# Strassen's weight sums in a transformer trunk: from VectorE to ScalarE negations and adding DMAs

## The chip, the cores and the metric

The kernel runs on one core of one Trainium2 chip. The metric is the device time of one execution in microseconds, as the median of several runs. The engines are TensorE (PE for its matmuls, PEld for its weight loads), VectorE (DVE), ScalarE (ACT), GpSimd (POOL) and SyncE (SP), which here only issues DMAs.

## The reference, cut to what matters

The reference is a trunk of two layers on 256 tokens of width 2048. Each layer has a mixer (attention of two kinds) and then a feed-forward block. The change touches only the feed-forward block:

```python
h = rms_norm(x, norm_mlp[i])
x = x + jnp.square(jax.nn.relu(h @ w_up[i])) @ w_down[i]
```

`w_up[i]` is 2048 x 8192, `w_down[i]` is 8192 x 2048, all in float32.

## The kernel before

**The stream of items.** The whole kernel is one list of items. An item is one block of weights of 256 rows by 512 columns (two row blocks of 128, held as a tile of 128 x 1024 elements, 512 KB) and the matmuls that use it. For each item the main loop (the end of `trunk`) does three things ahead of time. `load` issues, from SyncE, the DMA of the block into a tile `wraw` out of a ring of 5, seven items ahead. `split`, two items ahead, writes the block as the sum of two parts of reduced precision into a tile `w` out of a ring of 3: the high part by a ScalarE copy (`copy`, L89), the low part by a VectorE subtraction (L993). Then `mm` issues the matmuls, three for each product of 128 rows (high x high, high x low, low x high). An item whose `src` is empty is not loaded; its `form` says which tile is split instead. `early`, `after` and `post` are lists of further steps that are issued before an item's matmuls, after its split, and after its matmuls.

Since `w` has three buffers, the split of an item can begin when the matmuls three items before it are done.

**The down projection.** The hidden width of 8192 is taken in four parts f = 0 to 3 of 2048. For each f, `up(f)` computes the hidden features (lines L289 to L291, 16 items of 256 rows for each of four column blocks), and `down(f)` multiplies them with the rows of `w_down` of this part. `down(f)` takes the 2048 output columns in two pairs n = 0, 1 of two blocks G and H of 512 columns (`down_pair`). In the order of the program up(f + 1) stands before down(f). In the second layer the last pair (f = 3, n = 1) is done by plain items, so there are 15 pairs in all, 8 in the first layer and 7 in the second.

In each pair, six of the eight row blocks are plain: items G0 to G5 and H0 to H5 of 12 matmuls each (L427). The other two row blocks, `qa` and `qb` (0 and 2), form with the two column blocks and the two token blocks a 2 x 2 by 2 x 2 product, computed by Strassen's scheme in a form due to Winograd: seven items s1 to s7 of six matmuls each (`seventh`, L446) instead of eight. Four of them multiply blocks of w_down as they are, b11 (rows qa, columns G), b12 (qa, H), b21 (qb, G), b22 (qb, H), or sums of them:

| item | weights |
|---|---|
| s1, s2, s3 | b11, b21, b22 |
| s5 | b12 - b11 up to sign |
| s7 | b22 - b12 up to sign |
| s6 | b11 + b22 - b12 up to sign |
| s4 | b21 - (s6's sum) up to sign |

The left factors are blocks of the hidden features or sums of them, which `sums` computes on VectorE ahead of each f. The results of s5, s6, s7 and s1 are added to the residual `xs` by VectorE (`p1` to `p7`, L466, L482). Those of s2, s3 and s4 go on top of the sums of the plain items.

The order of the items in a pair is written out by hand:

```python
TURNS = "G0 s1 G1 H0 s5 G2 H1 s7 G3 H2 G4 s6 H3 s3 s2 H4 s4 G5 H5".split()
```

**The block sums before.** `load_block` loads b11, b22, b21 and b12 from SyncE into four tiles of their own, issued 8, 6, 5 and 3 items before the pair begins. When an s item is split, `minus` (L489) first makes the difference of two blocks on VectorE, in place of one of them, and `b4` (L494) makes the one for s4 after the split of s6. The s items read these tiles, so they have no `wraw` of their own.

Within the down projection instructions that go through `keep` stay in program order on their engine; for the others the scheduler of the framework picks the order on each engine when the program is built, so that an instruction may stand earlier than it was written. The matmuls' order is fixed.

## Time and profile before

| | |
|---|---|
| median of 3 runs | 2077.85 us (2077.53 to 2077.92) |
| the profiled execution's own time | 2077.52 us |
| its span | 2075.8 us |
| TensorE busy | 2062.2 us (99%) |
| VectorE busy | 1467.0 us (71%) |
| ScalarE busy | 1026.2 us (49%) |
| GpSimd busy | 26.3 us (1%) |
| granted TensorE clock | 1.00 |
| read from HBM | 425.90 MB |

A row of a timeline gives start, duration, engine, line, operation, output and inputs, the number of instructions merged into it, and in brackets how long the engine was idle before and what ended that. PE and PEld are TensorE's matmuls and weight loads. A row of the waits gives the waiting engine and line, what it waited for, the total in us, how often, and the longest. In the tables by line a bar separates busy time and mean duration (in ns) from the idle time before. Transfers are told by the median time from issue to landing. The ends of matmuls are modelled, so how long a matmul really occupied TensorE is seen from the distance of the starts.

In rows on the order of instructions, numbers behind a tile's name tell buffers apart, sizes are partitions x elements, and semaphores in brackets are what an instruction waits for: DMASW for transfers issued by GpSimd, DMAHW for those of SyncE, and the engines by name.

### The profile page before, as it was taken

What the parts mean: (1) busy time and instruction counts of PE and PEld (TensorE: products, weight loads), DVE (VectorE), ACT (ScalarE), POOL (GpSimd) and SP (SyncE); (2) the same over time, 40 slices, a digit from 0 to 9 for tenths busy, and PEclk for the clock granted to TensorE, in tenths of its full rate; (3) what the DMA queues carried; (4) which work ended last, traced back from release to release, by engine and by line L of the source; (5) the groups of instructions that cost most, each with busy time, mean ns of one, the idle gap of its engine ahead of it and who ended that gap; (6) DMA issues with size and microseconds to landing.
All of it is one profiled execution on the core that took longest, in us unless ns stands there. A gap on an engine that the chain in (4) does not pass through costs nothing.

```text
span 2075.8 us, 24805 instructions
## 1 busy us (share of the span) xinstructions
PE 2062.2 (99%) x9164; PEld 1696.1 (82%) x9164; DVE 1467.0 (71%) x1611; ACT 1026.2 (49%) x1233; POOL 26.3 (1%) x71
## 2 busy tenths in 40 slices
PE   9999999999999999999999999999999999999999
PEld 7888888888888888888887788878888888888887
DVE  5556555666696687688885898666669668867885
ACT  6555554544444454445554566554445444444453
POOL 0100000000000000000000000000000000000000
PEclk9999999999999999999999999999999999999999
DMA  9787856988766966876679688498876687677655
GB/s 305 229 235 213 236 172 199 298 250 245 219 208 216 256 206 209 233 211 209 200 216 264 184 250 258 143 265 271 246 242 205 212 238 221 209 216 224 204 176 165
DMA packets 477466, 464.83 MB, mean 224 GB/s; under 512 B 269665, under 2 KB 279969, under 8 KB 477345
## 3 DMA queue, kind: packets, MB, share of 16 engines
q1 hardware_dynamic: 469488, 455.81, 72.3%
q10 hardware_dynamic: 7856, 7.45, 1.2%
q8 instruction: 71, 1.16, 0.2%
q14 instruction: 51, 0.41, 0.1%
HBM read 425.90 MB, written 37.22 MB: 223 GB/s over the span
## 4 chain that ended last, share of the span: by engine, by line
PE 88%; DVE 6%; DMA 2%; issue 2%; ACT 1%; SPq 1%; DVEq 0%; ACTq 0%
PE acc L290 20%; PE acc L291 20%; PE acc L289 20%; PE acc L427 19%; DVE w L993 3%; PE aux L446 2%; DVE xs L466 2%; PE acc L446 1%; ACT w L89 1%; SPq L175 1%; DMA td<-jx 1%; PE acc L259 1%; PE aux L858 1%; DMA wraw<-in_w_up_dram 1%; DVE u L482 0%
## 5 line engine op out<-in xcount | busy, mean ns | idle before, releaser
L993 DVE TENSOR_TENSOR w<-wraw,w 128x1024 fp32r<-128x1024 f32 (+1 forms) x680 | 826.8, 1217 | 506.8 <-ACT w L89 502.0
L89 ACT ACTIVATE w<-wraw 128x1024 fp32r<-128x1024 f32 (+1 forms) x680 | 720.5, 1060 | 860.4 <-PE acc L291 565.0
L290 PE MATMUL acc<-w,xT 128*128 128x512 f32 x1632 | 638.1, 391 | 1.7 <-DVE w L993 1.5
L289 PE MATMUL acc<-w,xT 128*128 128x512 f32 x1632 | 637.1, 391 | 1.9 <-ACT xT L200 1.0
L291 PE MATMUL acc<-w,xT 128*128 128x512 f32 x1632 | 636.3, 390 | 0.0
L427 PE MATMUL acc<-w,hT 128*128 128x512 f32 x2160 | 512.3, 390 | 4.4 <-DVE w L993 3.4
L427 PEld LDWEIGHTS acc<-w,hT 128*128 128x128 f32 x2160 | 404.0, 188 | 96.1 <-DVE w L993 12.4
L289 PEld LDWEIGHTS acc<-w,xT 128*128 128x128 f32 x1632 | 306.4, 188 | 66.8 <-ACT w L89 2.1
L290 PEld LDWEIGHTS acc<-w,xT 128*128 128x128 f32 x1632 | 306.4, 188 | 66.5 <-DVE w L993 2.7
L291 PEld LDWEIGHTS acc<-w,xT 128*128 128x128 f32 x1632 | 306.4, 188 | 64.1 <-issue 0.7
L89 ACT ACTIVATE w<-b 128x1024 fp32r<-128x1024 f32 x105 | 111.5, 1062 | 83.9 <-PE acc L427 61.1
L993 DVE TENSOR_TENSOR w<-b,w 128x1024 fp32r<-128x1024 f32 x105 | 127.8, 1217 | 26.8 <-ACT w L89 26.8
L289 PE MATMUL acc<-w,oT 128*128 128x512 f32 x256 | 100.3, 394 | 0.0
L290 PE MATMUL acc<-w,oT 128*128 128x512 f32 x256 | 99.5, 390 | 0.0
L291 PE MATMUL acc<-w,oT 128*128 128x512 f32 x256 | 99.0, 391 | 0.0
L446 PE MATMUL aux<-w,S 128*128 128x512 f32 x270 | 68.5, 389 | 0.0
L446 PEld LDWEIGHTS aux<-w,S 128*128 128x128 f32 x270 | 50.7, 188 | 10.5
L289 PEld LDWEIGHTS acc<-w,oT 128*128 128x128 f32 x256 | 48.1, 188 | 10.2 <-ACT junk L796 0.4
L290 PEld LDWEIGHTS acc<-w,oT 128*128 128x128 f32 x256 | 48.1, 188 | 9.8
L291 PEld LDWEIGHTS acc<-w,oT 128*128 128x128 f32 x256 | 48.1, 188 | 9.8
L489 DVE TENSOR_TENSOR b<-b,b 128x1024 f32<-128x1024 f32 x45 | 54.8, 1217 | 0.2
L169 DVE STREAM_TRANSPOSE jx<-acc 128x512 f32<-128x512 f32 x68 | 44.6, 694 | 12.0 <-PE acc L291 9.2
(176 smaller groups left out, 1200.0 us busy)
## 6 DMA issues: line engine op xcount, KB each, us to landing
wraw<-in_w_up_dram SPq DMA_DIRECT2D x256, 512.0 KB, 4.4
wraw<-in_w_down_dram SPq DMA_DIRECT2D x196, 512.0 KB, 4.7
wraw<-in_w_in_a_dram SPq DMA_DIRECT2D x94, 512.0 KB, 4.6
wraw<-in_w_in_b_dram SPq DMA_DIRECT2D x64, 512.0 KB, 4.6
td<-jx SPq DMA_DIRECT2D x240, 128.0 KB, 4.3
b<-in_w_down_dram SPq DMA_DIRECT2D x60, 512.0 KB, 4.9
jx<-td SPq DMA_DIRECT2D x45, 512.0 KB, 6.1
wraw<-in_w_out_a_dram SPq DMA_DIRECT2D x32, 512.0 KB, 3.7
```

Source lines behind the costliest of these rows:

```text
L89: pin(act.activation(o, i, AF.Copy, scale=scale))
L169: dve.transpose(y[:, m:m + k, :].rearrange("p k f -> p (k f)"), part)
L175: keep(nc.sync.dma_start(d[:, :, :, a, :].rearrange("b j n i -> j n b i"), y[32 * a:32 * a + 32].rearrange("p n (b i) -> p n b i", b=4)))
L259: pin(pe.matmul(accs[key][t], L[:, j, part, t * P:(t + 1) * P], wx[:, j, :], start=(j == 0 and n == 0), stop=False))
L289: pin(pe.matmul(acc[t], L[:, k, 0, ts], wh[:, j, :], start=(k == 0), stop=False))
L290: pin(pe.matmul(acc[t], L[:, k, 0, ts], wl[:, j, :], start=False, stop=False))
L291: pin(pe.matmul(acc[t], L[:, k, 1, ts], wh[:, j, :], start=False, stop=(k == (end if t else KT) - 1)))
L427: keep(pe.matmul(acc[t], L[:, k, part, ts], wx[:, j, :], start=(i, j, m) == (0, 0, 0), stop=(i, j, m) == (len(qs) - 1, KB - 1, 2)))
L446: keep(pe.matmul(p, left(part, j), wx[:, j, :], start=to is None and (j, m) == (0, 0), stop=to is None and (j, m) == (KB - 1, 2)))
L466: dve.scalar_tensor_tensor(xc, p, sec["rs2"][:, t:t + 1], xc, op0=OP.mult, op1=OP.add)
L489: dve.tensor_sub(x, block(a), block(b))
L993: pin(dve.tensor_sub(wl[:, a], raw[:, a], wh[:, a].bitcast(F32)))
```

## The change

The sums of weight blocks are made in another way. For each pair there are two tiles, tx and ty, in two sets for n = 0 and n = 1 (the same room as the four tiles before).

- s1, s2 and s3 become ordinary items: their blocks come in the stream of `wraw`.
- 11 items before the pair, SyncE loads b12 into ty (`load_block`). At 8 items, ScalarE writes -ty into tx and then -ty into ty (`negate`, an ACTIVATE with scale -1). At 7 items, two DMAs issued by GpSimd with an accumulate operation add b11 to tx and b22 to ty, from DRAM (`gather`). tx is then s5's sum and ty s7's.
- After the split of s7, another adding DMA adds b11 to ty, which makes s6's sum.
- After the split of s6, ScalarE writes -ty into tx, and an adding DMA adds b21: s4's sum.
- In `sums`, the signs of two left blocks are turned (two `scalar_tensor_tensor` in place of an add and a subtraction), since the signs of the weight sums differ from before.

The items, their order and the matmuls are the same. The core of the diff:

```diff
-        def load_block(name, f, n, col, q):
-            b = sec[name, n % 2] = sec["pool"].tile([P, KB, 512], F32, name=name, bufs=1)
-            nc.sync.dma_start(b, rows(w_down[l], 2048 * f + KB * P * q, KB * P,
-                                      1024 * n + 512 * col, 512))
+        def block_rows(f, n, col, q):
+            return rows(w_down[l], 2048 * f + KB * P * q, KB * P, 1024 * n + 512 * col, 512)
...
-            dve.tensor_add(b4[:, 0], a21, a22)
-            dve.tensor_sub(b4[:, 1], b4[:, 0], a11)
+            dve.scalar_tensor_tensor(b4[:, 0], a21, -1.0, a22, op0=OP.mult, op1=OP.subtract)
+            dve.scalar_tensor_tensor(b4[:, 1], b4[:, 0], -1.0, a11, op0=OP.mult, op1=OP.subtract)
...
-                it = Item(None, KB, 512, mm, True)
-                it.form = form
+                it = Item(None if callable(form) else form, KB, 512, mm, True)
+                it.form = form if callable(form) else None
...
-            def minus(out, a, b, then=None):
-                def form():
-                    x = block(out)
-                    dve.tensor_sub(x, block(a), block(b))
-                    return x
-                return form
-
-            def b4():
-                dve.tensor_sub(block("b12"), block("b21"), block("b11"))
-
             qa, qb = SEVEN
+
+            def raw(col, q):
+                return block_rows(f, n, col, q)
+
+            def load_block():
+                for name in ("tx", "ty"):
+                    sec[name, half] = sec["pool"].tile([P, KB, 512], F32, name=f"{name}{half}", bufs=1)
+                nc.sync.dma_start(block("ty"), raw(1, qa))
+
+            def negate(out, i):
+                act.activation(block(out), block(i), AF.Copy, scale=-1.0)
+
+            def gather(out, col, q):
+                nc.gpsimd.dma_start(block(out), raw(col, q), accum_op=OP.add)
+
+            def t1_t3():
+                negate("tx", "ty")
+                negate("ty", "ty")
+
+            def add_t1_t3():
+                gather("tx", 0, qa)
+                gather("ty", 1, qb)
+
+            def t4():
+                negate("tx", "ty")
+                gather("tx", 0, qb)
+
             seven = {
-                "s1": seventh(own(qa, 0), lambda: block("b11"), None, p1),
-                "s2": seventh(own(qb, 0), lambda: block("b21"), (0, 0)),
-                "s3": seventh(summed(3), lambda: block("b22"), (1, 0)),
-                "s4": seventh(own(qb, 1), lambda: block("b12"), (0, 1)),
-                "s5": seventh(summed(0), minus("b11", "b12", "b11"), None, p5),
-                "s6": seventh(summed(1), minus("b11", "b22", "b11"), None, p6),
-                "s7": seventh(summed(2), minus("b12", "b22", "b12"), None, p7)}
-            seven["s6"].after = b4
+                "s1": seventh(own(qa, 0), raw(0, qa), None, p1),
+                "s2": seventh(own(qb, 0), raw(0, qb), (0, 0)),
+                "s3": seventh(summed(3), raw(1, qb), (1, 0)),
+                "s4": seventh(own(qb, 1), lambda: block("tx"), (0, 1)),
+                "s5": seventh(summed(0), lambda: block("tx"), None, p5),
+                "s6": seventh(summed(1), lambda: block("ty"), None, p6),
+                "s7": seventh(summed(2), lambda: block("ty"), None, p7)}
+            seven["s7"].after = lambda: gather("ty", 0, qa)
+            seven["s6"].after = t4
...
-            for name, col, q, at in (("b11", 0, qa, 8), ("b22", 1, qb, 6), ("b21", 0, qb, 5), ("b12", 1, qa, 3)):
-                items[base - at].early.append(lambda name=name, col=col, q=q: load_block(name, f, n, col, q))
+            for at, step in ((11, load_block), (8, t1_t3), (7, add_t1_t3)):
+                items[base - at].early.append(step)
```

In the changed kernel the lines behind the change are shifted: the low parts are L1009, the copies L89 as before, the negations L495, the adding DMAs L498, the adds of the results L464 and L480, and the sums of the left blocks begin at L393.

## The prediction

> **What bounds the kernel now.** The page first: the span, the engines' shares, and the chain that ended last.
>
> ```profile
> span 2075.8 us, 24805 instructions
> PE 2062.2 (99%) x9164; PEld 1696.1 (82%) x9164; DVE 1467.0 (71%) x1611; ACT 1026.2 (49%) x1233; POOL 26.3 (1%) x71
> PE 88%; DVE 6%; DMA 2%; issue 2%; ACT 1%; SPq 1%; DVEq 0%; ACTq 0%
> ```
>
> TensorE is busy 99% of the span and holds the chain. What work VectorE does costs nothing unless TensorE waits for it. The list of waits says how much that is in the plain down items (L427): the weight loads waited 12.4 us for VectorE's low parts.
>
> ```profile
> PEld acc L427 <- DVE w L993: 12.4, 19, 1.2
> ```
>
> So the down pairs were cut out one by one in the table of windows, each window from a pair's first matmul to the next one's (columns: length, busy time and count of PE, PEld, DVE, ACT, POOL, granted clock, DMA share, GB/s). Five of the fifteen, the sum, and one stretch of up items:
>
> ```profile
> 390.98:559.62 168.64, 168.64 (x745) 139.67 (x744) 105.75 (x111) 74.67 (x75) 0.00 (x0) 1.00 0.86 254
> 602.29:645.00 42.71, 42.60 (x188) 34.97 (x187) 35.38 (x35) 20.73 (x20) 0.00 (x0) 1.00 0.61 200
> 731.90:774.58 42.68, 42.51 (x187) 34.83 (x186) 39.14 (x38) 22.61 (x22) 0.00 (x0) 1.00 0.69 219
> 904.20:947.95 43.75, 42.82 (x188) 34.75 (x186) 41.51 (x43) 22.61 (x22) 0.00 (x0) 1.00 0.67 213
> 1033.10:1077.20 44.10, 43.16 (x188) 34.78 (x187) 40.66 (x47) 26.26 (x36) 0.00 (x0) 1.00 0.68 191
> 1899.73:1943.48 43.75, 42.85 (x188) 34.76 (x187) 41.50 (x43) 22.61 (x22) 0.00 (x0) 1.00 0.65 209
> sum 643.55, PE 639.19 PEld 522.84 DVE 565.56 ACT 330.72 POOL 0.00; mean PE 42.61 PEld 34.86 DVE 37.70 ACT 22.05 POOL 0.00
> 619.97 8.32 PE L427 MATMUL acc<-w,hT 128*128 128x512 f32 x36
> ```
>
> The last row, from the timeline, gives the step of TensorE: 36 matmuls in 8.32 us, the last one lasting 0.39, so (8.32 - 0.39)/35 = 0.2266 us each. A pair has 12 plain items of 12 matmuls and 7 Strassen items of 6, 186 in all, so 186 x 0.2266 = 42.15 us is the least it can take, and fifteen take 632.2. They took 643.6. **All that any relief of VectorE can win in the pairs is 11 us, 0.5%.** VectorE is nearly full there (41.5 of 43.75 us), ScalarE half full, GpSimd empty.
>
> Where the 11 us lie: most pairs lose about 0.5 us (42.7 against 42.15), three lose more: the two of 43.75 (f = 2, n = 0, once in each layer) and the one of 44.10 (first layer, f = 3, n = 1). The timeline of the first of them, around s5 and G2:
>
> ```profile
> 908.65 1.22 DVE L489 TENSOR_TENSOR b<-b,b 128x1024 f32<-128x1024 f32 x1
> 911.58 1.21 DVE L993 TENSOR_TENSOR w<-b,w 128x1024 fp32r<-128x1024 f32 x1
> 912.71 1.22 DVE L353 TENSOR_TENSOR hT<-jx,hT 128x1024 fp32r<-128x1024 f32 x1
> 913.85 1.22 DVE L395 TENSOR_TENSOR jx<-hT 128x1024 f32<-128x1024 f32 x1
> 914.99 1.22 DVE L993 TENSOR_TENSOR w<-wraw,w 128x1024 fp32r<-128x1024 f32 x1
> 916.26 2.14 PE L427 MATMUL acc<-w,hT 128*128 128x512 f32 x8 [0.76 <-DVE w L993]
> ```
>
> VectorE runs without a gap, with a block difference (L489) in the queue, and the low part of the next item comes a microsecond late. The common stall, near each pair's end, is of another kind:
>
> ```profile
> 629.42 1.23 DVE L993 TENSOR_TENSOR w<-b,w 128x1024 fp32r<-128x1024 f32 x1 [1.49 <-ACT w L89]
> 630.57 0.68 DVE L482 TENSOR_TENSOR u<-aux,u 128x512 f32<-128x512 f32 x1
> 631.17 1.21 DVE L993 TENSOR_TENSOR w<-b,w 128x1024 fp32r<-128x1024 f32 x1
> 632.30 1.94 DVE L466 SCALAR_TENSOR_TENSOR xs<-u,rs,xs 128x512 f32<-128x512 f32 x2
> 634.16 1.22 DVE L993 TENSOR_TENSOR w<-wraw,w 128x1024 fp32r<-128x1024 f32 x1
> 635.43 2.37 PEld L427 LDWEIGHTS acc<-w,hT 128*128 128x128 f32 x11 [0.54 <-DVE w L993]
> ```
>
> Here VectorE was idle 1.49 us just before. The short items s3 and s2 (1.36 us each) come together with the adds of s6's result (L482, L466), and no block difference is near.
>
> **The change, part by part.** *Differences leave VectorE.*
>
> ```profile
> L489 DVE TENSOR_TENSOR b<-b,b 128x1024 f32<-128x1024 f32 x45 | 54.8, 1217 | 0.2
> L494 DVE TENSOR_TENSOR b<-b,b 128x1024 f32<-128x1024 f32 x15 | 18.3, 1220 | 0.3
> L89 ACT ACTIVATE w<-b 128x1024 fp32r<-128x1024 f32 x105 | 111.5, 1062 | 83.9 <-PE acc L427 61.1 <-PE acc L291 9.9 <-PE aux L446 8.5
> ```
>
> 60 instructions of 1.22 us go, 73 us. On the path they are worth only the three odd pairs: 43.75 - 42.68 = 1.1 us twice, and 44.10 - 42.71 = 1.4 once, of which I take 1.1, since that window reaches a little into the next section: 3.3 at most. But in the two pairs of 43.75 the order on VectorE changes too. Before, around the stall (w: a low part; jx from hT: the sum for the left blocks):
>
> ```order
> L993 TENSOR_TENSOR w_6605<-wraw_6513,w_6605 128x1024
> L466 SCALAR_TENSOR_TENSOR xs_89<-aux_6610,rs2_3153,xs_89 128x512
> L993 TENSOR_TENSOR w_6622<-b11_6435,w_6622 128x1024
> L353 TENSOR_TENSOR hT_6297<-jx_6527,hT_6297 128x2x4x128
> L395 TENSOR_TENSOR jx_7143<-hT_6297 128x1024
> L993 TENSOR_TENSOR w_6640<-wraw_6549,w_6640 128x1024
> ```
>
> Now, the same place:
>
> ```order
> L1009 TENSOR_TENSOR w_6622<-wraw_6532,w_6622 128x1024
> L464 SCALAR_TENSOR_TENSOR xs_89<-aux_6627,rs2_3153,xs_89 128x512
> L393 TENSOR_TENSOR jx_7170<-hT_6313 128x1024
> L1009 TENSOR_TENSOR w_6638<-tx0_6396,w_6638 128x1024
> L353 TENSOR_TENSOR hT_6313<-jx_6546,hT_6313 128x2x4x128
> L1009 TENSOR_TENSOR w_6656<-wraw_6566,w_6656 128x1024
> ```
>
> The sum for the left blocks moved ahead of s5's low part. Three instructions still stand between H0's and G2's low parts, and this sum must also wait for its buffer. So the gain there is 0 to 1.1 us a pair, and I take half: 1.1 + 1.1 = 2.2 us in all. The common stall stays, since its rows hold nothing that is removed.
>
> *ScalarE gains 45 negations.* At the 1.06 us of its copies that is 3.2 us a pair on 21 to 23 us of 42.7: hidden by its idle time. The rewritten sums (8 times two short VectorE instructions) cost nothing that can be seen beside VectorE's new 4.9 us of room a pair. Of the loads, 60 into b become 15 into ty and 45 in the ordinary stream; the number from SyncE is the same, about 16 a pair.
>
> *60 accumulating transfers from GpSimd are new,* 512 KB each, four a pair. Two are needed only a pair later. The last one (for s4) follows a negation at about 622.9 in the pair shown and is needed at 633.8, over 9 us later. The tight one is between s7 and s6. ScalarE's queue there before, and now:
>
> ```order
> L89 ACTIVATE w_4603<-wraw_4532 128x1024 [waits DMAHW4_49,DVE_49,PE_49]
> L89 ACTIVATE w_4621<-b11_4361 128x1024 [waits DVE_49,PE_49]
> L89 ACTIVATE w_4637<-wraw_4563 128x1024 [waits DMAHW5_49,DVE_49,PE_49]
> ```
>
> Now ty holds s7's block and then, after the transfer, s6's:
>
> ```order
> L89 ACTIVATE w_4611<-wraw_4536 128x1024 [waits DMAHW3_49,DVE_49,PE_49]
> L495 ACTIVATE tx1_4311<-ty1_4312 128x1024 [waits DMASW0_49]
> L89 ACTIVATE w_4628<-ty1_4312 128x1024 [waits DVE_49,PE_49]
> L89 ACTIVATE w_4645<-wraw_4567 128x1024 [waits DMAHW4_49,DVE_49,PE_49]
> ```
>
> The negation for s4 now stands in front of s6's copy and waits for the transfer (DMASW0); behind it queue s6's copy, H3's, and all that follow, and behind those TensorE. On GpSimd the second pair's transfer stands behind those of a later pair, (waits named as semaphores):
>
> ```order
> L498 DMA tx0_5181<-in_w_down_dram 128x2x512 [waits DMASW5_49,Activation_49]
> L498 DMA ty0_5182<-in_w_down_dram 128x2x512 [waits DMASW4_49,Activation_49]
> L498 DMA ty1_4312<-in_w_down_dram 128x2x512 [waits DMASW3_49,DMASW0_49,DVE_49]
> L498 DMA tx1_4311<-in_w_down_dram 128x2x512 [waits DMASW1_49,Activation_49]
> ```
>
> Those negations stand a dozen instructions further up, so they do not hold it. The transfer's time allowance, from the timeline of that pair:
>
> ```profile
> 615.57 1.22 DVE L993 TENSOR_TENSOR w<-b,w 128x1024 fp32r<-128x1024 f32 x1
> 622.89 1.06 ACT L89 ACTIVATE w<-b 128x1024 fp32r<-128x1024 f32 x1 [1.65 <-PE acc L427]
> 623.99 1.23 DVE L993 TENSOR_TENSOR w<-b,w 128x1024 fp32r<-128x1024 f32 x1 [0.53 <-ACT w L89]
> 628.13 1.52 PE L446 MATMUL aux<-w,S 128*128 128x512 f32 x6
> ```
>
> s7's low part ends at 616.79; then GpSimd may issue. ScalarE takes up s6 at 622.89, its low part ends at 625.22, 2.33 later, and TensorE wants it at 628.13. With the negation (1.06) in front, the transfer must have landed by 628.13 - 2.33 - 1.06 = 624.74. The allowance is 624.74 - 616.79 = **8.0 us**; each microsecond more stalls TensorE by one, fifteen times.
>
> No transfer of this kind is in the trace. The nearest rows:
>
> ```profile
> q1 hardware_dynamic: 4417, 8.52, 60.4%
> DMA to landing us min/median/max: 3.7/4.9/10.6
> jx<-td SPq DMA_DIRECT2D x45, 512.0 KB, 6.1
> ```
>
> The first is the pair of 602.29 to 645.00: 0.604 x 42.71 = 25.8 us of all sixteen DMA engines for 8.52 MB, 1.6 us per 512 KB. The second is the plain 512 KB load of a block (b), the third one that moves 512 KB in small packets. Below, the transfer costs what a plain load does, 4.9. It reads its target too, so I count the 1.6 us twice: 4.9 + 1.6 = 6.5. Above, its 3.2 us must fit into the 40% that the queue of SyncE leaves free: 3.2/0.4 = 8.0, and 4.9 - 1.6 = 3.3 around it: 11.3. I take 7.2, nearer to the rows of 4.9 and 6.1 than to that end: in time, with 0.8 us to spare. As plain loads scatter up to 10.6, I put one transfer in fifteen as late by a microsecond: +1.0 us.
>
> The Trainium skill, page "DMA: Bandwidth & Descriptors", section "Anatomy of one DMA", gives 2.0 us plus the bytes at 436 GB/s for a DMA from GpSimd, an estimate of 3.2 us for 512 KB and 4.4 with both operands; by it nothing is ever late and the sum would be 2075.6. The plain load's 4.9 us here is above that already, so the rows are kept.
>
> **Sum.** The profiled execution took 2077.52 us (1.7 around the span), 0.33 below the median of 2077.85. 2077.52 - 2.2 + 1.0 = 2076.3; on the median **2076.6**.
>
> **Rivals.**
> - *The transfer is late in every pair* (slower). It decides at 8.0 us; from 8.45 on the loss, 15 x 0.45 = 6.8, passes the gain by over 0.2% of the time. At 10 us: 15 x 2.0 = 30, less 2.2, 2105.7; at 11.3: 49.5, 2125. For it: DMA shares of 0.6 to 0.7 and the double work. Against: 6.5 from the rows. 0.31.
> - *GpSimd is shut out while VectorE runs,* and issues only at an instruction's end, 1.2 us late at most since VectorE's instructions follow without gaps after 615.57: 7.2 + 1.2 = 8.4, so 15 x 0.4 = 6, and 1.0 for the scatter, less 2.2: 2082.6. The Trainium skill, page "SBUF — State Buffer", section "Who interferes with whom", states such a lock for VectorE's two-port modes, and that tensor_tensor has none; no run here shows GpSimd issuing beside VectorE. 0.07.
> - *The DMA engines fill up.* Four transfers of 3.2 us add 0.30 to shares of 0.58 to 0.71, up to 1.0, and the weight stream is late: 2 us in each of eight pairs, 16 less 2.2: 2092. Against: 0.86 in the up items at 390.98 without a lost microsecond. 0.05.
> - *VectorE's load was behind the common stall too.* All 11.3 us go: 2066.5. For it: VectorE's 35 to 41 us a pair. Against: its idle 1.49 us before the stall. 0.07.
> - The forecast: 0.50.
>
> **How the numbers follow.** 0.2%, 4.2 us, is about what a measurement of this kernel can tell. Same 0.50 (forecast), slower 0.31 + 0.07 + 0.05 = 0.43, faster 0.07. The forecast's own range is 2074.5 (3.3 won, nothing late) to 2081. The range of all: the late case reaches 2108 at 10.15 us; what lies beyond (0.13) and the last rival (0.07) are left out. Low end 2072, between the forecast's and the last rival's.
>
> **What would show it.** Right: no L489 or L494, ScalarE's wait at L495 for the transfer under 2 us (from 622.89 to 624.74), the ty transfer's landing near 7 us, pairs of 42.6 us, and the common stall still there. Wrong: pairs above 43.2 us with TensorE waiting at s6 and ScalarE idle at L495 for DMA; or the common stall gone.

## The result, and the profile after

The changed kernel takes **2097.6 us** (median of 4 runs, 2096.9 to 2100.5) against 2077.9 for the kernel before on the same chip: a ratio of 1.0096, 95% interval 1.0078 to 1.0113. It is 1% slower, against a forecast of 2076.6 us. The profiled execution has a span of 2096.3 us, 20.5 more than before.

The page first: the span, the engines, the transfers by queue (packets, MB, share of sixteen engines' span), and the chain.

```profile
span 2096.3 us, 25022 instructions
PE 2067.1 (99%) x9164; PEld 1698.4 (81%) x9164; DVE 1401.7 (67%) x1551; ACT 1068.1 (51%) x1278; POOL 99.0 (5%) x131
q1 hardware_dynamic: 469488, 455.81, 71.1%
q0 software_dynamic: 16320, 31.46, 9.3%
PE 88%; DVE 4%; DMA 4%; issue 3%; ACT 1%; SPq 1%; ACTq 0%; DVEq 0%
```

VectorE has 65 us less to do, ScalarE 42 more. TensorE still holds the chain. The new entry is q0: 60 transfers, 31.46 MB, and 9.3% of all sixteen DMA engines.

Where the 20 us lie is found by setting the start of each of the 9164 matmuls against the start of the same matmul before. Six places hold nearly all of it:

| place | lost, us |
|---|---|
| start of the feed-forward section, first layer | 6.1 |
| start of the feed-forward section, second layer | 8.2 |
| pair f=0 n=0, first layer | 0.6 |
| pairs f=2 n=0, both layers | 1.7 and 2.1 |
| pair f=3 n=1, first layer | 1.4 |

14 of 20 us are lost where no pair is near. The table of windows, one row of 30 us and one of 35 for the two section starts, shows it in the count of matmuls (the first number in parentheses). Before:

```profile
391.00:421.00 30.00, 30.00 (x134) 24.86 (x133) 17.57 (x27) 13.61 (x17) 0.00 (x0) 1.00 0.90 278
1395.00:1430.00 35.00, 33.45 (x145) 26.80 (x144) 21.31 (x25) 16.92 (x21) 0.00 (x0) 1.00 0.88 265
```

After:

```profile
391.00:421.00 30.00, 26.07 (x107) 20.87 (x106) 11.67 (x20) 14.53 (x19) 5.02 (x4) 0.94 1.00 267
1395.00:1430.00 35.00, 27.32 (x109) 21.42 (x108) 17.62 (x30) 17.87 (x26) 4.85 (x4) 0.90 1.03 285
```

134 matmuls became 107, and 27 x 0.2266 = 6.1 us; 145 became 109, 8.2 us. GpSimd has four instructions in each window: four adding transfers, those of the first two pairs, which are not needed for another 170 us and more. The changed kernel's order on ScalarE shows how they came there (the names are those of the first pairs' tiles):

```order
L495 ACTIVATE tx0_3966<-ty0_3967 128x1024 [waits DMAHW3_49]
L89 ACTIVATE w_2979<-wraw_2869 128x1024 [waits DMAHW0_49,PE_49]
L495 ACTIVATE tx1_4311<-ty1_4312 128x1024 [waits DMAHW4_49,Pool_49]
L495 ACTIVATE ty0_3967<-ty0_3967 128x1024 [waits Activation_49]
L495 ACTIVATE ty1_4312<-ty1_4312 128x1024 [waits Activation_49]
```

The tiles tx and ty of both sets are free when the section opens, the negations are not kept in program order, and so the scheduler put all of them at the section's start, and the transfers follow as soon as their negations are done. What that did to the DMA engines is in the view of transfers for the first 15 us of the section (queues as above; below, what was issued and its median time to landing). Before:

```profile
q1 hardware_dynamic: 5843, 3.76, 90.8%
wraw<-in_w_up_dram SPq DMA_DIRECT2D x5, 512.0 KB, 6.1
```

After:

```profile
q0 software_dynamic: 684, 1.34, 51.0%
q1 hardware_dynamic: 4724, 1.61, 44.9%
...
wraw<-in_w_up_dram SPq DMA_DIRECT2D x5, 512.0 KB, 15.2
tx<-in_w_down_dram POOLq DMA_DIRECT2D x2, 512.0 KB, 8.6
ty<-in_w_down_dram POOLq DMA_DIRECT2D x2, 512.0 KB, 15.5
```

Before, the DMA engines were already 91% busy there. The adding transfers took half of them, SyncE's queue fell from 3.76 to 1.61 MB, and the weight blocks landed after 15.2 us instead of 6.1 (medians of five). The timeline of the second section's start shows how that reaches TensorE:

```profile
1398.60 2.50 POOL L498 DMA_DIRECT2D tx<-in_w_down_dram  x2 [330.20 <-ACT tx L495]
...
1400.84 1.49 POOL L498 DMA_DIRECT2D ty<-in_w_down_dram  x1
...
1402.14 11.79 SPq L990 DMA_DIRECT2D wraw<-in_w_up_dram  x4
...
1402.73 1.20 POOL L498 DMA_DIRECT2D ty<-in_w_down_dram  x1 [0.40 <-ACT rs_y L223]
...
1416.37 1.06 ACT L89 ACTIVATE w<-wraw 128x1024 fp32r<-128x1024 f32 x1 [10.25 <-DMA wraw<-in_w_up_dram]
...
1417.47 0.79 PE L289 MATMUL acc<-w,xT 128*128 128x512 f32 x1 [6.44 <-ACT w L89]
```

ScalarE waited 10.25 us for one weight block, and TensorE 6.44 for ScalarE. Around these stalls the matmuls also ran at half the clock for a while, as the windows (column before the last two: granted clock) of the two places show:

```profile
412.25:415.67 3.42, 3.42 (x10) 2.67 (x9) 1.17 (x1) 1.63 (x2) 0.00 (x0) 0.50 1.05 402
1415.77:1422.60 6.83, 4.66 (x10) 3.38 (x11) 3.68 (x3) 3.18 (x3) 0.00 (x0) 0.50 1.04 391
```

Now the pairs, from the same table of windows. They answer to the rows of before at 559.62 (a pair of 42.67), 602.29, 904.20, 1033.10 and 1899.73:

```profile
565.67:608.91 43.24, 42.46 (x188) 34.84 (x187) 35.13 (x34) 25.43 (x25) 4.85 (x4) 1.00 0.85 234
608.91:651.47 42.56, 42.45 (x187) 34.84 (x186) 30.87 (x31) 23.65 (x23) 4.84 (x4) 1.00 0.90 247
910.81:956.22 45.41, 43.37 (x187) 34.61 (x186) 37.44 (x39) 25.30 (x25) 4.85 (x4) 1.00 0.83 221
1041.37:1086.86 45.49, 43.39 (x187) 34.68 (x186) 36.19 (x43) 27.06 (x37) 2.42 (x2) 1.00 0.88 241
1917.59:1963.45 45.86, 43.26 (x187) 34.61 (x186) 37.43 (x39) 25.34 (x25) 4.81 (x4) 1.00 0.83 223
```

The pair that the prediction worked on (second row) is unchanged. The two of f=2 n=0, which were to win 1.1 us each, lost. In the rows shown, the DMA share of a pair was 0.61 to 0.69 before and is 0.83 to 0.90 now. The timeline of the pair in the third row, and then of the fourth, in which s6 was late:

```profile
918.51 1.23 DVE L393 TENSOR_TENSOR jx<-hT 128x1024 f32<-128x1024 f32 x1 [1.79 <-DMA td<-jx]
919.65 1.22 DVE L1009 TENSOR_TENSOR w<-tx,w 128x1024 fp32r<-128x1024 f32 x1
...
926.52 1.22 DVE L1009 TENSOR_TENSOR w<-ty,w 128x1024 fp32r<-128x1024 f32 x1
...
934.58 1.06 ACT L495 ACTIVATE tx<-ty 128x1024 f32<-128x1024 f32 x1 [3.37 <-DMA ty<-in_w_down_dram]
...
946.80 2.79 PE L425 MATMUL acc<-w,hT 128*128 128x512 f32 x11 [1.22 <-DVE w L1009]
...
1054.65 1.22 DVE L1009 TENSOR_TENSOR w<-ty,w 128x1024 fp32r<-128x1024 f32 x1
...
1065.49 1.06 ACT L495 ACTIVATE tx<-ty 128x1024 f32<-128x1024 f32 x1 [2.39 <-DMA ty<-in_w_down_dram]
...
1068.81 1.43 PE L444 MATMUL aux<-w,S 128*128 128x512 f32 x5 [0.77 <-DVE w L1009]
```

First, VectorE stood 1.79 us at the left sum (L393), which waited for its buffer, with s5's low part (919.65) behind it. Then ScalarE stood 3.37 us at the negation for s4 (L495), waiting for the adding transfer. The stall in front of H4 (946.80) grew from the common 0.33 us to 1.39. (Here and below, a stall of TensorE is the distance between the starts of two matmuls, less the step of 0.2266 us.) In the other pair s7's low part ended at 1055.87, the transfer let ScalarE go at 1065.49, 9.6 us later, and TensorE stalled 1.4 us at s6 and 1.2 at H3 behind it.

### The profile page after: what moved, and what is told of

It is laid out like the page before. It is cut to its first block, busy times and chain, and to the rows that moved or that the text cites. A ratio compares the mean times of both kernels' runs of the same rounds, so it can differ in the third digit from the quotient of the medians.

```text
span 2096.3 us, 25022 instructions
## 1 busy us (share of the span) xinstructions
PE 2067.1 (99%) x9164; PEld 1698.4 (81%) x9164; DVE 1401.7 (67%) x1551; ACT 1068.1 (51%) x1278; POOL 99.0 (5%) x131
## 3 DMA queue, kind: packets, MB, share of 16 engines
q0 software_dynamic: 16320, 31.46, 9.3%
## 4 chain that ended last, share of the span: by engine, by line
PE 88%; DVE 4%; DMA 4%; issue 3%; ACT 1%; SPq 1%; ACTq 0%; DVEq 0%
PE acc L290 20%; PE acc L289 20%; PE acc L291 20%; PE acc L425 20%; PE aux L444 3%; DVE w L1009 2%; DMA wraw<-in_w_up_dram 1%; ACT w L89 1%; DMA ty<-in_w_down_dram 1%; PE acc L444 1%; DVE xs L464 1%; SPq L175 1%; PE aux L874 1%; DVE u L480 0%; DMA wraw<-in_w_in_a_dram 0%
## 5 line engine op out<-in xcount | busy, mean ns | idle before, releaser
L1009 DVE TENSOR_TENSOR w<-wraw,w 128x1024 fp32r<-128x1024 f32 (+1 forms) x725 | 881.0, 1218 | 584.2 <-ACT w L89 579.1
L89 ACT ACTIVATE w<-wraw 128x1024 fp32r<-128x1024 f32 (+1 forms) x725 | 767.3, 1060 | 881.1 <-PE acc L291 570.8
L498 POOL DMA_DIRECT2D ty<-in_w_down_dram x30 | 38.2, 1291 | 999.2 <-DVE w L1009 998.5
L498 POOL DMA_DIRECT2D tx<-in_w_down_dram x30 | 36.2, 1208 | 656.2 <-ACT tx L495 656.1
L289 PEld LDWEIGHTS acc<-w,oT 128*128 128x128 f32 x256 | 48.1, 188 | 10.2 <-ACT junk L812 0.4
L495 ACT ACTIVATE tx<-ty 128x1024 f32<-128x1024 f32 x30 | 31.8, 1061 | 44.9 <-DMA ty<-in_w_down_dram 37.9
L1009 DVE TENSOR_TENSOR w<-ty,w 128x1024 fp32r<-128x1024 f32 x30 | 36.6, 1221 | 26.8 <-ACT w L89 26.8
```

The lines of the kernel that those rows point to most:

```text
L89: pin(act.activation(o, i, AF.Copy, scale=scale))
L289: pin(pe.matmul(acc[t], L[:, k, 0, ts], wh[:, j, :], start=(k == 0), stop=False))
L495: act.activation(block(out), block(i), AF.Copy, scale=-1.0)
L498: nc.gpsimd.dma_start(block(out), raw(col, q), accum_op=OP.add)
L1009: pin(dve.tensor_sub(wl[:, a], raw[:, a], wh[:, a].bitcast(F32)))
```

## The experiments

The theory after reading these profiles: the loss is made at the section starts by the doubled DMA work of the early adding transfers, and the rest in four pairs by the transfer between s7 and s6 and by the left sum. The main rivals: that transfer is late in every pair; GpSimd's requests as such cost, adding or not; the negations on ScalarE cost; the pairs lose by VectorE's load. Ratios are to the kernel before on the same chip, with 95% intervals.

**1. The first steps in place.**

```diff
             def t1_t3():
-                negate("tx", "ty")
-                negate("ty", "ty")
+                keep(negate("tx", "ty"))
+                keep(negate("ty", "ty"))
```

> The first negations of each pair are kept at their written place on ScalarE, so the first two pairs' four adding transfers leave the start of each feed-forward section; their loads into ty stay early. Theory (the section starts are the loss: +6.1 us in the first layer and +8.0 in the second against the kernel before, because the four early adding transfers fill the DMA engines while the weight stream is short): both starts fall to within 1 us of before, 2097.6 - 14.1 = 2083.5 us, and no stall of more than 1.5 us there. Rival (the transfer between s7 and s6 is late in every pair): nothing changes, 2097 us or more. What the pairs lose in the theory (about 6 us in four of them) stays.

2097.6 us, 1.0094 (1.0079 to 1.0109): as the rival had it, and yet not for its reason. Windows of this kernel, the section starts first, then two pairs (f=0 n=0 and f=2 n=0):

```profile
391.00:421.00 30.00, 30.00 (x134) 24.86 (x133) 17.74 (x27) 13.60 (x17) 0.00 (x0) 1.00 0.82 254
1395.00:1430.00 35.00, 35.00 (x156) 29.00 (x155) 21.33 (x33) 20.08 (x32) 0.00 (x0) 1.00 0.91 303
559.78:605.26 45.48, 43.45 (x187) 34.60 (x186) 36.57 (x36) 25.75 (x26) 4.81 (x4) 1.00 0.97 278
909.77:957.52 47.75, 44.30 (x187) 35.92 (x186) 37.10 (x39) 24.80 (x25) 4.82 (x4) 0.96 0.93 255
```

The starts came back whole: 134 matmuls as before, and at the second one 156 where the kernel before had 145. But the steps of all pairs were moved, not those of the first alone. Each n=0 pair still issues four adding transfers, but its own first two now run right in front of it (issued at 540.56 and 541.64 for the pair that begins at 559.78), and those for the n=1 pair behind it run in its middle (589.68 and 591.58), where the changed kernel issues its last two near the pair's end (601.96 and 603.05, for a pair from 565.67 to 608.91). The DMA share of the six n=0 pairs of f=0 to 2 rose to 0.92 to 0.98, and each became 2.6 to 4.0 us longer than in the kernel before. In the first of them the transfer between s7 and s6 landed after 8.5 us instead of 6.8 in the changed kernel, and the stalls are at s6 (0.6 us, 0.4 at the item behind it) and at H4 (1.4). The loss had moved to where the DMA engines were full next. As an undoing of one part it was too broad; the fifth experiment mends that.

**2. s6's sum in tx.**

```diff
+            def t6():
+                act.activation(block("tx"), block("ty"), AF.Copy)
+                gather("tx", 0, qa)
             def t4():
-                negate("tx", "ty")
-                gather("tx", 0, qb)
+                negate("ty", "tx")
+                gather("ty", 0, qb)
...
-            seven["s7"].after = lambda: gather("ty", 0, qa)
+            seven["s5"].after = t6
```

(s4 then reads ty and s6 tx.)

> s6's sum is made in tx instead of ty, started right after s5's split, so that its adding transfer no longer waits for s7's low part and has some 20 us instead of 8; s4's sum then goes into ty. All else is as changed, the early transfers at the section starts included. Theory (about 4 to 5 of the 20 us come from that transfer being late in four pairs: the H4 stalls of f=0 n=0 and f=2 n=0 and the stalls of f=3 n=1): 2092 to 2094 us, those pairs shorter by 0.5, 1.2, 1.2 and 2.8 us, section starts as they are. Rival (that transfer is what costs everywhere): 2078 us. Rival (the pairs lose by VectorE's order, the left sums placed early): pairs unchanged, 2097 us.

2118.1 us, 1.0192 (1.0171 to 1.0214), against all expectations. The timeline of the first pair:

```profile
584.13 1.06 ACT L495 ACTIVATE ty<-tx 128x1024 f32<-128x1024 f32 x1 [3.91 <-DMA tx<-in_w_down_dram]
585.09 2.00 ACT L89 ACTIVATE w<-wraw 128x1024 fp32r<-128x1024 f32 x2
...
586.19 0.50 PE L425 MATMUL acc<-w,hT 128*128 128x512 f32 x1 [0.28 <-ACT w L89]
...
587.45 0.73 PE L425 MATMUL acc<-w,hT 128*128 128x512 f32 x2 [0.76 <-DVE w L1013]
```

The scheduler had placed the negation for s4 (L495) ahead of s6's copy again, and here even ahead of the copies of the two plain items before it, H2 and G4. It stood there 3.91 us waiting for the transfer, and the splits behind it made TensorE wait. More time for the transfer is worth nothing while an instruction that waits for it stands in the queue of the splits.

**3. The transfers do not add.**

```diff
-                nc.gpsimd.dma_start(block(out), raw(col, q), accum_op=OP.add)
+                nc.gpsimd.dma_start(block(out), raw(col, q))
```

> The 60 transfers from GpSimd lose their accumulate operation and only write: the same queue, the same number, the same bytes from DRAM; the sums of the blocks are left out. Theory (an adding transfer takes twice the DMA engines' time; at a section start the transfers then amount to 2 + 2 x 4 = 10 block times against 4 in the kernel before, and 6 block times of 1.6 us = 9.7 us is about what the weight stream loses): with 2 + 4 = 6 block times only 3.2 us of the engines' time is extra, so the starts lose 0 to 3 us each, and the landing between s7 and s6 falls from about 7.8 to 5 to 6 us, in time: 2077 to 2085 us. Rival (the number of transfers, or GpSimd's issuing, is what costs): 2095 us or more.

2082.5 us, 1.0017 (1.0007 to 1.0027): about four fifths of the loss gone, with the same number of transfers and bytes at the same places. From the view of one line, the transfers' time to landing (min, median, max) in the changed kernel, and then the same and the queue's row in this one:

```profile
DMA to landing us min/median/max: 5.7/7.9/17.0
```

```profile
DMA to landing us min/median/max: 4.0/6.5/9.3
q0 software_dynamic: 8640, 31.46, 4.9%
```

The same 31.46 MB took 4.9% of the DMA engines, not 9.3%. The first theory's point that adding doubles the work, and that this is what the starts have no room for, stands. The windows of the starts show 129 and 143 matmuls, 5 and 2 fewer than in the kernel before.

**4. No transfers at all.**

```diff
-                nc.gpsimd.dma_start(block(out), raw(col, q), accum_op=OP.add)
+                pass
```

> The 60 transfers from GpSimd are left out, the negations on ScalarE stay (the sums of the blocks are left out). Theory: both section starts as in the kernel before, no pair waits at L495, VectorE still without its 60 differences: 2074.5 to 2077.5 us; the two pairs of f=2 n=0 keep a stall of about 0.5 us from the left sum. Rival (the four negations at the section start delay the splits on ScalarE): the starts still lose 6 and 8 us, 2090 us or more.

2076.1 us, 0.9992 (0.9983 to 1.0002). The starts show 134 and 156 matmuls although the negations stand at the same places: ScalarE's part in the loss is excluded. The pairs f=2 n=0 of this kernel:

```profile
903.75:947.85 44.10, 43.04 (x187) 34.68 (x186) 37.43 (x39) 25.51 (x25) 0.00 (x0) 1.00 0.71 209
1898.64:1943.04 44.40, 43.07 (x188) 34.69 (x186) 37.44 (x39) 25.50 (x25) 0.00 (x0) 1.00 0.69 208
```

Here VectorE is relieved and nothing else is added, and these two pairs are still 0.4 and 0.7 us longer than before (43.75). What relieving VectorE wins was seen only in f=3 n=1 of the first layer, 0.65 + 0.74 us, where two stalls behind differences are gone. (The second section's start also gained 1.1 us, which the eleventh experiment puts down to the loads.)

**5. The first pairs' transfers moved, alone** (with the loads and negations that go ahead of them).

```diff
             def t1_t3():
-                negate("tx", "ty")
-                negate("ty", "ty")
+                for out in ("tx", "ty"):
+                    ins = negate(out, "ty")
+                    if f == 0:
+                        keep(ins)
...
-                items[base - at].early.append(step)
+                items[base - at - (32 if f == 0 else 0)].early.append(step)
```

> As changed, but for the first pairs of each section alone (f=0) the negations are kept in program order and written 32 items further ahead (40 before the pair, among the first up items), so their four adding transfers run neither at the section's start nor in the pairs; all later pairs as changed. Theory (the section starts cost 14 us because of where these four transfers run; the first experiment gave the starts back but put the early transfers of all pairs beside the late ones): starts as in the kernel before, pairs as in the changed kernel with their 6 us of loss: 2083.5 us, 2081.5 to 2085. Rival (moving adding transfers only moves the loss, wherever they go): 2095 us or more.

2081.7 us, 1.0012 (1.0002 to 1.0021). The section starts:

```profile
391.00:421.00 30.00, 30.00 (x134) 24.86 (x133) 17.88 (x27) 13.61 (x18) 0.00 (x0) 1.00 0.82 253
1395.00:1430.00 35.00, 35.00 (x156) 29.01 (x155) 22.86 (x31) 17.33 (x23) 0.00 (x0) 1.00 0.83 262
```

Both are whole, and the four transfers of each section, now in two twos among the up items (issued at 453.77, 454.86, 505.48 and 508.09 in the first layer), cost nothing, although the DMA share from 421 to 480 us rose from 0.86 to 0.95. A high share alone is therefore not the cause. Two things differ from the section's start: two transfers come at a time and not four, and the weight stream has run for 60 us. No experiment took these two apart. The pairs kept their loss (45.99 and 45.01 us for f=2 n=0). Moving eight adding transfers of sixty took the slowdown from 0.96% to 0.12%; by the traces, from 20.0 to 4.6 us.

**6. Time for s6, without a waiting negation in the way.** The fifth and the second together, and in `split` the copies of items that have an `after` step are kept:

```diff
+            was, pinned[0] = pinned[0], pinned[0] or it.after is not None
             copy(wh[:, a], raw[:, a])
+            pinned[0] = was
...
-                negate("tx", "ty")
+                keep(negate("ty", "tx"))
```

> The first pairs' transfers early as in the fifth experiment, and s6's sum made in tx right after s5's split as in the second one, but with the copies of s5 and s6 and the negation for s4 kept in program order, so that this negation stands behind s6's copy and no split queues behind it waiting for the transfer. Theory (what the second experiment lost was that negation, put 4 us ahead of the transfer's landing, and what the pairs lose in the changed kernel is the transfer between s7 and s6): the H4 stalls of 0.9 to 1.4 us fall to the common 0.33, f=3 n=1 loses its 2.8: 2077 to 2079 us. Rival (two adding transfers in the middle of a pair are too much for the DMA engines, with whatever time allowance): pairs of 43 us or more and 2085 us.

2077.1 us, 0.9993 (0.9984 to 1.0002): the total shows no loss any more. By the matmul starts the pairs still lose 2.8 us against the kernel before, and the second section's start gives 2.4 of it back. The stall at H4 is 0.33 in f=0 n=0 and in both pairs f=2 n=0. f=3 n=1 of the first layer still has 2.6 us of stalls, so the theory's gain of 2.8 there did not come: it is not the transfer between s7 and s6 alone that is late at the layer's end.

**7. The left sum late as well.**

```diff
-            dve.tensor_add(a, hi.bitcast(F32), lo.bitcast(F32))
+            keep(dve.tensor_add(a, hi.bitcast(F32), lo.bitcast(F32)))
```

> The sixth experiment's kernel, with the first addition of each left sum also kept in program order on VectorE, so that in f=2 n=0 it no longer stands in front of s5's low part. Theory (the stalls of 0.4 to 1.0 and 0.8 us before s5 and G2 in these two pairs are this sum's waiting for its buffer): both pairs at 42.7 us, 3.3 us less than the sixth: 2074 to 2076 us, under the kernel before. Rival (they are VectorE's load at that place, whatever the order): as the sixth.

2076.7 us, 0.9988 (0.9978 to 0.9998). Both pairs f=2 n=0:

```profile
905.28:947.91 42.63, 42.46 (x187) 34.84 (x186) 34.12 (x33) 25.97 (x26) 3.65 (x4) 1.00 0.84 237
1900.80:1943.42 42.62, 42.45 (x187) 34.84 (x186) 34.12 (x33) 26.37 (x26) 3.83 (x4) 1.00 0.86 245
```

They fell to 42.6, as the theory had it; the total is a little above the range that was written. 1.6 us came back in the first layer as a stall at G1 of f=3 n=0, behind the sums' new place.

**8. The kernel before, with the same one line kept.**

> The kernel before, with nothing changed but that first addition of the left sums kept in program order: no adding transfers, VectorE with its 60 differences. Theory (of the three odd pairs, two are odd by the order of VectorE's instructions and not by its load): both pairs of 43.75 us fall to 42.7, 2075.8 us, so that most of what relieving VectorE could win is had by order alone. Rival (VectorE's load of 41.5 us in the pair is the reason): unchanged, 2077.9 us.

2078.2 us, 0.9994 (0.9985 to 1.0004): the total is not told apart from the kernel before, but the two pairs are:

```profile
904.12:946.77 42.65, 42.48 (x187) 34.83 (x186) 39.15 (x38) 22.60 (x22) 0.00 (x0) 1.00 0.70 214
1901.31:1943.95 42.64, 42.47 (x187) 34.83 (x186) 39.15 (x38) 22.61 (x22) 0.00 (x0) 1.00 0.71 219
```

43.75 became 42.65 with VectorE still doing all its differences: the two odd pairs were odd by order. Of these 2.2 us 1.5 were lost again: in each layer a stall of 0.6 us came at G1 of f=3 n=0, and those pairs became 0.7 and 0.8 us longer.

**9. Only the eight transfers at the starts do not add.**

```diff
-            def gather(out, col, q):
-                nc.gpsimd.dma_start(block(out), raw(col, q), accum_op=OP.add)
+            def gather(out, col, q, **kw):
+                nc.gpsimd.dma_start(block(out), raw(col, q), **(kw or {"accum_op": OP.add}))
...
             def add_t1_t3():
-                gather("tx", 0, qa)
-                gather("ty", 1, qb)
+                how = {"accum_op": OP.bypass} if f == 0 else {}
+                gather("tx", 0, qa, **how)
+                gather("ty", 1, qb, **how)
```

> As changed, with every transfer at its place, but the four early transfers of the first pairs in each section only write and do not add (the sums of the first pairs' blocks are left out); all others add. Theory (at the section starts it is the doubled work of adding that the DMA engines have no room for): the starts go as in the third experiment, +0.7 us in place of +6.1 in the first layer and about -0.6 in place of +8.0 in the second against the kernel before, and the pairs stay as changed: 2083.5 us, 2082 to 2087. Rival (it is the four extra requests from GpSimd at that place, adding or not): 2095 us or more.

2088.3 us, 1.0050 (1.0037 to 1.0062), a little above the range that was written. The starts:

```profile
391.00:421.00 30.00, 28.94 (x127) 23.33 (x126) 16.15 (x26) 16.81 (x21) 3.06 (x4) 1.00 0.91 300
1395.00:1430.00 35.00, 33.00 (x142) 26.06 (x141) 20.66 (x31) 19.75 (x27) 2.95 (x4) 1.00 0.95 320
```

7 and 3 matmuls fewer than before, 1.6 and 0.7 us (1.0 by the starts of the second layer), where the adding ones lost 6.1 and 8.2. Nothing was changed but the operation of eight transfers.

**10. Sums three items earlier.** The seventh with `items[-7].post` instead of `items[-4].post` for `sums(3)`.

> The seventh experiment's kernel, with the left sums of f=3 written three items earlier (7 items before the end of the pair ahead instead of 4), since in that kernel the pairs that follow, f=3 n=0, show a stall of 1.6 and 0.7 us at their third item. Theory (the burst of left sums on VectorE just before the pair causes it): these stalls go, 2 us less than the seventh: a ratio to the kernel before of 0.997 to 0.999. Rival (the burst stalls the pair ahead instead): no change against the seventh, 0.9988.

2093.5 us, 1.0075 (1.0062 to 1.0089). The edit missed its aim: seven items before the end stands ahead of s3 in the list, so s3 of f=2 n=1 took the left sums of f=3, which are not its own, and waited 6.9 us for them, in both layers, with 10.2 us of halved clock around each stall. It says nothing on the burst of sums.

**11. The kernel before, its loads in place.** The eighth, and the loads into b kept in order on SyncE:

```diff
-            nc.sync.dma_start(b, rows(w_down[l], 2048 * f + KB * P * q, KB * P,
-                                      1024 * n + 512 * col, 512))
+            keep(nc.sync.dma_start(b, rows(w_down[l], 2048 * f + KB * P * q, KB * P,
+                                           1024 * n + 512 * col, 512)))
```

> The kernel before with the left sum late as in the eighth experiment, and the plain loads of the blocks kept in program order on SyncE, so that the first pair's four no longer stand at the section's start. Theory (what is loaded early costs at a section start even when it is plain: the kernel before stalls 2.15 us at the second one, the kernels with two early loads do not): the second start gains 2 us, 2075 us, a ratio of 0.9985. Rival (the second start's stall in the kernel before has nothing to do with these loads): as the eighth, 2078 us.

2082.0 us, 1.0019 (1.0011 to 1.0028). The matmuls around the second section's start gained 2.4 us on the kernel before, which has stalls of 0.8, 1.0 and 0.3 us there: four plain early loads cost about that much, and two, as in the fifth to seventh, nothing. But against the eighth the six n=0 pairs of f=0 to 2 all lost (43.1 to 44.6 us each), with new stalls at G1 and H0, so the total went the rival's way. Moved to its written place, a transfer costs there.

**12. Sums one item earlier.** The seventh with `items[-5].post`.

> The seventh experiment's kernel with the left sums of f=3 written one item earlier only (behind s2 of the pair ahead, so that s3 still reads the old sums; in the tenth they stood ahead of s3, which therefore waited for the new ones). Theory (the stall of 1.6 and 0.7 us at the third item of f=3 n=0 is the burst of left sums on VectorE ahead of it, which then has one item of 2.7 us more room): these stalls go, about 2 us less than the seventh, a ratio to the kernel before of 0.997 to 0.999. Rival (the burst only moves): no change against the seventh's 0.9988.

2076.3 us, 0.9986 (0.9977 to 0.9995), against 0.9988: the stall at G1 of f=3 n=0 went from 1.6 to 0.9 us in the first layer, and the total is not told apart from the seventh. (The 0.7 us of the expectation lie at G1 of f=1 n=1 of the second layer in the seventh's trace, so the burst of sums has no part in them.) With it, the change with its transfers out of the way is about 0.14% faster than the kernel before. By the matmul starts of the profiled execution, what is won lies elsewhere than in VectorE's relief: 2.0 us at the second section's start, where two early loads are gone, and 1.1 in each pair f=2 n=0, which the eighth had by order alone. The 1.4 us of relief in f=3 n=1 (fourth experiment) are there too, but f=3 n=0 and f=3 n=1 of the first layer are 3.9 us longer all the same. By the eighth, the order of the left sum, which needs no change of method, is worth about 1 us of those 3 (an estimate, since neither of the two intervals excludes the other).

## Why the prediction was wrong, point by point

The measured 2097.6 us lie inside the prediction's whole range, 2072 to 2108, but by luck: the range reaches so far for a transfer that is late at s6 in every pair, and it was late enough to stall s6 in one pair of fifteen.

- **"All that any relief of VectorE can win in the pairs is 11 us"** was not contradicted: no kernel here came more than 3 us below the one before.
- **"I take half: 1.1 + 1.1 = 2.2 us in all"** was too much. The fourth experiment, with VectorE relieved and no transfer, won 1.4 us of it in the pairs, all in f=3 n=1, and its pairs f=2 n=0 lost 0.4 and 0.7. The 43.75 us there were put down to VectorE's load; the eighth showed that they were its order. The sum ahead of s5's low part, whose move the prediction quoted, made it worse, because it waits 1.79 us for its buffer. "0 to 1.1 us a pair" left out that end below nothing.
- **"The common stall stays"** held: 0.33 us in the fourth, sixth and seventh experiments.
- **"Hidden by its idle time"** (ScalarE's 45 negations) held, by the fourth experiment.
- **"I take 7.2"** for the landing was near: the median of all is 7.9, and of the transfer between s7 and s6 in the pair worked out it was 6.55 from the end of s7's low part. The 1.6 us counted twice were right: 9.3% of 2096.3 us over 60 transfers is 3.25 us of all the DMA engines for each, and 1.70 without adding (4.9% of 2081.3). The allowance of **8.0 us** was right too: the pair with 9.6 us stalled 1.4 us at s6, the others 0.1 at most. What was mis-sized was the price of being nearly late. "One transfer in fifteen as late by a microsecond: +1.0" looked at s6 alone. In f=0 n=0 the negation was let go 7.1 us after the low part, in time for s6, and yet H4's stall behind it grew by 0.6, since all that ScalarE and VectorE do next comes later. The pairs lost 5.8 us in all, 1.7 and 2.1 of them with the left sum's part. The Trainium skill's fit in "DMA: Bandwidth & Descriptors", section "Anatomy of one DMA", gives an estimate of 3.2 us for these bytes; the trace shows 5.7 at the least.
- **"Two are needed only a pair later"** is the step that failed. It priced two of each pair's four transfers at nothing because nobody waits for them. Nobody did, and still eight of them cost 14 of 20 us, by what they took from others: the DMA engines, in the two stretches right at the sections' starts, where the share was 0.88 to 0.91 before (the windows above) and SyncE's weight blocks then came too late (15.2 us instead of 6.1 in the first layer). The fifth experiment moved these eight and took the loss at the starts away; the ninth left them there without adding and took most of it away. The order on GpSimd and ScalarE was read at the pairs and not at the section's start, where nothing held the first pairs' steps back.
- **"The DMA engines fill up"** was the right rival, given 0.05 and the wrong place. It was put aside by "0.86 in the up items at 390.98 without a lost microsecond". That row is a mean over 168.64 us; its first 15 us were at 0.91 before, in the queue's row above. Had the window been cut there, the prediction's own prices would have given the size: four adding transfers of 3.2 us, less two plain loads of 1.6 that are no longer early, less the 9% of 15 us that was free, is 12.8 - 3.2 - 1.4 = 8.2 us at a start (an estimate made after the fact), against 6.1 and 8.2 measured.
- **"GpSimd is shut out while VectorE runs"** falls. In the changed kernel's timeline GpSimd issued 0.30 us after s7's low part ended (623.70 after 623.40) and kept its 1.20 us beside VectorE's next instruction, which began at 623.80. The Trainium skill, "SBUF — State Buffer", section "Who interferes with whom", says that tensor_tensor has no two-port mode and contends with GpSimd only over GpSimd's reads; this row, an issue beside a tensor_tensor, agrees.

How the 14.3 us at the starts divide can be read from the matmul starts: in the stretches of half the clock each matmul came 0.20 us later than at the full one, 1.6 us in the first layer and 1.8 in the second; the other 11 us are waits for late weights.

What stays open: why the end of the first layer (f=3 n=1) keeps stalls of 1.2 to 2.8 us in all in every kernel with adding transfers, though the fourth experiment without them has none but the common one.

## What to carry to other kernels

A transfer that nobody waits for is not free: look where the scheduler will put it, and what the DMA engines carry in that stretch, in windows of some 15 us, as here, and not as long as a stage. When a wait gets a place in the queue of an engine that feeds TensorE, its slack is that of everything queued behind it. And before an engine is relieved, see whether its stalls are load or order: here one instruction kept in its place did for two of the three odd pairs what moving 60 instructions to other engines did not, though two thirds of that gain were lost again at the next place in VectorE's queue.

## What the runs showed of the hardware that was not expected

- An adding transfer of 512 KB into SBUF took more than twice the DMA engines' time of the same transfer without adding: 9.3% against 4.9% of their span for the same 60 transfers, 2048-byte packets of 178 ns (median) where the plain ones had 4096-byte packets of 159. GpSimd's issue took 1.20 us each, against 0.72 (medians of the changed kernel and of the third experiment).
- Transfers of GpSimd's queue held back those of SyncE's: at the first section's start the weight blocks landed after 15.2 us instead of 6.1, the adding transfers themselves after 8.6 and 15.5.
- The granted clock fell to a half around stalls of TensorE of 3.3 and 6.6 us in the changed kernel and 6.9 us in the tenth experiment, and stayed there for 3.41, 6.83 and 10.24 us, multiples of about 3.41. In the first experiment stalls of 2.7 and 2.3 us were enough (3.41 us of half clock each), while one of 2.5 us in the fifth left the clock whole, so the length of a stall alone does not decide it. The Trainium skill, "TensorE: Matmul & The Clock Gate", section "Part 1: The HAM clock gate", has the clock halved after an idle window of about 3.4 us; the stalls of 6.6 and 6.9 agree, and those of 2.3 to 3.3 show that less can do.
